# Three weight pairs computed as plain products at the start, stores on another queue, and first loads of each stage issued earlier

## The chip, the cores and the metric

The kernel runs on one core of a Trainium2 chip. The metric is the device time of one execution in microseconds (us); the median of the runs is what is compared. Before the change it is 1601.59 us, the median of three runs (1600.45 to 1611.41).

## The reference, cut to what matters

One layer of a block over 2048 tokens of width 1024, all in float32:

```
h    = rmsnorm(x) * g                                   # per token
proj = h @ w_in                                         # 1024 -> 6144 columns
q, k, v, z_att, B, C, u, z_conv, g_att, g_conv = split(proj)
att  = chunked attention: 64-token chunks, each sees itself and 8 before it, 8 heads, relative bias
ya   = (att * silu(z_att)) @ w_att_out                  # 512 -> 1024
yc   = (B * conv3_causal(C * u) * silu(z_conv)) @ w_conv_out
m    = sigmoid(g_att) * ya + sigmoid(g_conv) * yc
out  = rmsnorm(x + m @ w_out) * final_g
```

## The kernel before, in words

Every float32 matmul is done as three matmuls of rounded parts: weights and tokens are each split into a high part (a cast, on ACT) and a low part (the difference, on DVE), and high x high, high x low and low x high are summed in one PSUM bank (`passes`, L130 to L135). A *product* below is 4 contraction tiles x 3 such matmuls of 128x512, so 12 matmuls.

**The first projection.** The 6144 columns are 48 tiles of 128, taken two at a time: 24 *pairs*. The tokens are worked in two halves of 1024, each two chunks of 512. A pair in a half is a 2x2x2 block product (two column tiles, two chunks, two halves of the contraction), done by a Strassen-Winograd scheme with seven products instead of eight. `operand(p, i)` (L374) makes the weight operand i of pair p: raw weights come in two loads of 512 KB (`load_raw`), sums and differences are formed on DVE (L389 to L395), the result is split (`split_into`, L118) into one of four tiles of the pool `wr`. In the first half each operand is also stored to DRAM (L397, 512 KB, queued on SP two products later) and in the second half it is read back from there (L380). `operand_steps` (L346) makes the seven token operands of a half, in seven steps of four splits. `seq` (L536 to L543) is the list of all products by pair and i; the loop from L594 goes through it. Operands are asked for two products ahead in the first half, three in the second.

The first four pairs ("early") start before the norm is known. Products 1 and 2, which take chunk 0 alone, are computed for all four pairs from tokens that are multiplied by g only (`raw_split`, L338); their result is multiplied by the inverse norm later (`scale_early`, L588). The other five products of these pairs take normalized tokens: the sums of squares on ACT (L291), the inverse square root on DVE (`newton`, 13 small instructions), its spread over PE (L90), the multiplication in place (`normalize`, L302), the differences (`third`, L333), then the steps.

An evicted product goes to the output's handler: the gate pairs to a tanh on ACT and a store from ACT's own queue, the others to stores on SP, queued one product later by `defer` and `tick` (L108, L111). The v pairs (`ev_v`) are first transposed by PE (L431) and then split on ACT (L435) and DVE (L436) at the same point.

**Attention** (`attention`, L138) is a generator of 130 stages; its loads and stores are on GpSimd's (POOL's) queue. It starts when the first half's pairs are done (`first.close()`, L691): 64 stages are interleaved with the second half's products from the third pair on, the rest with what follows (`pump`).

**The rest**, for each half of the tokens: `half_c` takes 16 items (8 of the convolution, 8 of attention), each with a weight tile (`raw_w`, L711), two gate tiles (`gate`, L722, from the pool `gp` with three buffers) and two products over the stored inputs `mid` (`load_mid`, L717; 16 loads of 256 KB for each group of 8 items). `half_d` is the output projection of 8 token blocks, each followed by the residual, the sum of squares on ACT (L817), `newton` on DVE and the final scaling (L821) and store. The loads for each `half_c` are asked for after what stands before it in the program.

The engines' orders come from a scheduler, by priority, from the order of the program; each engine and each DMA queue then runs its list strictly in order. An instruction that waits holds everything behind it on its engine.

Of the kernel before, what the change touches and what calls it, by code (L numbers as in the profile page):

```python
# [17 lines left out]
P = 128  # L18
# [15 lines left out]
EARLY = 4  # L34

ORDER = (1, 2, 6, 5, 7, 4, 3)
REST = ORDER[2:]
# [4 lines left out]
def block_kernel(ctx, tc, xb, xt, wp_in, wy, wo, bias, ng, fg, cw, cb, out):  # L42
# [63 lines left out]
    later = []  # L106

# [230 lines left out]
    def raw_split(i, j, t):  # L338

        g = ng_sb[:, 4 * (i - 1) + j:4 * (i - 1) + j + 1]  # L340
        hi, lo = slot("rawh"), slot("rawl")
        nc.scalar.activation(hi, t, AF.Identity, scale=g)
        nc.vector.scalar_tensor_tensor(lo, t, g, hi.bitcast(F32), op0=ALU.mult, op1=ALU.subtract)
        raw_ops[i, j] = (hi, lo)

    def operand_steps(half):  # L346

        b11, b12, b21, b22 = (blocks[half, c, k] for k in range(2) for c in range(2))
        order = (1, 2, 6, 5, 7, 4, 3) if half else (1, 6, 5, 7, 2, 4, 3)
        for i in order:  # L350
# [18 lines left out]
    def load_raw(p, n):  # L369
        r = ww.tile([P, 2, 4, P], F32, tag="w", name="wraw")  # L370
        raws[p, n] = r
        nc.sync.dma_start(r, wp_in[p, n])

    def operand(p, i):  # L374
# [4 lines left out]
        if p >= NPAIR:  # L379
            nc.sync.dma_start(w.bitcast(F32), wc_d[q][i])  # L380
            return
# [15 lines left out]
        defer(2, lambda: nc.sync.dma_start(wc_d[q][i], w.bitcast(F32)))  # L397
# [14 lines left out]
    def ev_q(pr):  # L412
        def ev(g, c, t):
            for s, x in enumerate(parts(t)):
                defer(1, lambda s=s, x=x: nc.sync.dma_start(q_d[pr][s][g], x))
        return ev

    def ev_k(pr):
        def ev(g, c, t):
            for s, x in enumerate(parts(t)):  # L420
                for o in range(2):
                    r = (1 - s) * DH
                    defer(1, lambda x=x, o=o, r=r: nc.sync.dma_start(k_d[2 * pr + o][g // 2][r:r + DH, g % 2 * CH:(g % 2 + 1) * CH], x[o * DH:(o + 1) * DH]))
        return ev

    def ev_v(pr):
        def ev(g, c, t):
            def turn():
                ps = dbank("vt")
                for b in range(4):  # L430
                    nc.tensor.transpose(out=ps[:, b * P:(b + 1) * P], in_=t[:, b * P:(b + 1) * P], identity=ident)  # L431
                for b in range(2):
# [5 lines left out]
                    for h in range(2):  # L438
                        n = g % 2 * 4 + 2 * b
                        defer(1, lambda h=h, v4=v4, n=n: nc.sync.dma_start(v_d[2 * pr + h][g // 2][:, n:n + 2, :], v4[:, :, h, :]))  # L440
# [11 lines left out]
    def ev_z(pr):  # L452
        def ev(g, c, z):
            t = silu2(z)
            defer(1, lambda: nc.sync.dma_start(z_d[pr][g], t))
        return ev

    def conv_pair(b):
# [27 lines left out]
        def gated(g, c, t):  # L486
# [3 lines left out]
            if seen[g] == 2:  # L490
                for s, x in enumerate(parts(cv.pop(c))):
                    defer(1, lambda s=s, x=x: nc.sync.dma_start(mid_d[1][b][s][g], x))
# [10 lines left out]
    mixed = [C, C + 1, G + 4, C + 2, C + 3, G + 5, C + 4, C + 5, G + 6, C + 6, C + 7, G + 7]  # L503
# [3 lines left out]
    early = names[:EARLY]  # L507
    assert early == list(range(EARLY))

    def reduce_bias(h, n):  # L510
# [5 lines left out]
        def go():  # L516
# [5 lines left out]
            defer(1, lambda: nc.sync.dma_start(bias_d[h][:, n * m:(n + 1) * m], t))  # L522

        defer(3, go)

# [7 lines left out]
    main = {p: 1 for p in names}  # L533


    seq = [(p, i) for p in (2, 3, 0, 1) for i in (1, 2)]  # L536
    for p in (0, 2):
        seq += together(early[p], early[p + 1], both)
    mid0, mid1 = names[EARLY:NPAIR - 2], names[NPAIR + 2:]
    seq += [(p, i) for p in mid0 for i in ORDER]  # L540
# [3 lines left out]

    fslot = lambda name: slot(name, F32)
    nc.sync.dma_start(ng_sb, ng)
    load_x(0, 0, 0, (0, 1))
    load_raw(2, 0)
    load_x(0, 0, 0, (1, 2, 4))
    load_x(0, 0, 1)  # L550
    load_raw(3, 0)
    tok = [load_tokens(0, 0, b, fslot) for b in range(4)]
    load_x(0, 1, 0)
    load_x(0, 1, 1)
    load_raw(0, 0)
    load_raw(1, 0)
# [5 lines left out]
    t0, t1 = tiles_of(0, 0), tiles_of(0, 1)  # L562
    operand(2, 1)
    for j in range(4):
        raw_split(1, j, t0[j])
    operand(2, 2)
    for j in range(4):
        raw_split(2, j, t0[4 + j])
    acc = acc_tile()
    for b in range(4):  # L570
        sums(acc, b, tok[b])
    y0 = rsqrt_mean(acc, 4)
    tok = [load_tokens(0, 1, b, fslot) for b in range(4)]
    acc = acc_tile()
    steps = operand_steps(0)
    built = []
    pending = []
    nw = 2
    rb = {}
    x1 = None  # L580
# [7 lines left out]
    def scale_early():  # L588
        p, t, u = pending.pop(0)
        nc.vector.tensor_mul(t, t, rb[0])  # L590
        nc.vector.tensor_mul(u, u, rb[0])
        evs[p][0](0, 0, t)

    for s, (p, i) in enumerate(seq):  # L594
        half = p // NPAIR
        n = names.index(p)
        if s in (2, 3):
            load_raw(s - 2, 1)
        elif s in (15, 16):
            for k in range(2):  # L600
                load_raw(s - 13, k)
        elif s == 25 or s > 25 and half == 0 and i == 1 and n + 1 < NPAIR:
            for k in range(2):
                load_raw(names[EARLY] if s == 25 else names[n + 1], k)
        ahead = 3 if half else 2
# [3 lines left out]
        if s == 2:  # L609
            for b in range(4):  # L610
                sums(acc, b, tok[b])
            y1 = rsqrt_mean(acc, 4)
        elif s == 4:
            rb[0] = inverse(y0, fslot)
            for k in range(4):
                normalize(t0[k], k, rb[0])
        elif s == 5:
            rb[1] = inverse(y1, fslot)
            for k in range(8):
                normalize(t1[k], k, rb[1])  # L620
        elif s == 6:
            for j in range(4):
                third(0, j)
            for k in range(2):
                built.append(next(steps))
        elif s == 7:
            for k in range(4, 8):
                normalize(t0[k], k, rb[0])
        if s >= 6 and pending:
            scale_early()  # L630
        if s >= 8 and half == 0 and len(built) < 7:
# [285 lines left out]
```

## Time and profile before

| | |
|---|---|
| median of three runs | 1601.59 us (1600.45 to 1611.41) |
| the profiled execution's own time | 1607.36 us |
| its span, first to last instruction | 1605.6 us |
| PE busy | 1531.8 us, 95% of the span |
| DVE busy | 1033.1 us, 64% |
| ACT busy | 676.9 us, 42% |
| POOL busy | 155.1 us, 10% |
| mean granted TensorE clock | 0.978 |
| DMA | 417.24 MB, 260 GB/s over the span |

The profiled execution lies 5.8 us above the median; what lies around its span is 1.8 us. PE's busy time holds matmuls at half clock too, so a stretch in which PE is busy and the clock is below 1.00 has lost time as well.

### The profile page before, as it was taken

To read this page: it belongs to the slowest core of one execution; us is meant where nothing else is said; L and a number is where in the kernel's file an instruction comes from. 1 tells how busy PE (TensorE), PEld (TensorE's weight loads), DVE (VectorE), ACT (ScalarE), POOL (GpSimd) and SP (SyncE) were. 2 spreads that over 40 slices of the span, in tenths; PEclk is the share of its full clock that TensorE was granted. 3 is DMA by queue.
4 is the path that set the end of the run, shared out by engine and by line. 5 is a ranking of instruction groups with operands and counts; after the bars stand their busy time and mean duration, and the time that the engine had idled before them with its cause. 6 is when DMAs were issued, how large, how long until landed. Compare 5 with 4: busy or idle time off the path is not lost.

```text
span 1605.6 us, 21714 instructions
## 1 busy us (share of the span) xinstructions
PE 1531.8 (95%) x7344; PEld 1264.1 (79%) x7344; DVE 1033.1 (64%) x2078; ACT 676.9 (42%) x1261; POOL 155.1 (10%) x294
## 2 busy tenths in 40 slices
PE   5789999999899999999999999999999999989997
PEld 3568888888777788888888888887788877878886
DVE  4987789797668645546565555535578776665544
ACT  5443353443235323334344444425567766532211
POOL 0000000000000101111111111101233222000000
PEclk7899999999999999999999999999999999999999
DMA  9398889988887978787888898898866658277231
GB/s 350 147 349 339 323 326 340 358 329 283 315 287 249 310 250 268 232 301 248 275 293 296 281 318 264 279 310 278 294 187 205 216 181 286 86 242 262 66 105 66
DMA packets 169054, 417.24 MB, mean 260 GB/s; under 512 B 20976, under 2 KB 41456, under 8 KB 168944
## 3 DMA queue, kind: packets, MB, share of 16 engines
q1 hardware_dynamic: 138736, 329.85, 59.3%
q0 software_dynamic: 20992, 69.22, 13.5%
q10 hardware_dynamic: 9216, 16.78, 2.7%
q8 instruction: 59, 0.97, 0.2%
q14 instruction: 51, 0.42, 0.1%
HBM read 253.77 MB, written 162.00 MB: 259 GB/s over the span
## 4 chain that ended last, share of the span: by engine, by line
PE 82%; DVE 9%; DMA 5%; ACT 2%; issue 2%; SPq 0%; DVEq 0%; POOL 0%; ACTq 0%
PE ps_d L135 21%; PE ps_d L133 21%; PE ps_d L134 21%; PE po L226 4%; PE ps_t L208 3%; PE ps_s L188 3%; PE ps_d L808 3%; PE ps_d L806 3%; PE ps_d L807 3%; DMA mid<-mid 2%; DVE ps_s L194 1%; DVE wc L121 1%; DVE ptl L214 1%; DMA gl<-gate 1%; DMA wc<-wc 1%
## 5 line engine op out<-in xcount | busy, mean ns | idle before, releaser
L156 POOL DMA_DIRECT2D q<-q x128 | 66.6, 528 | 828.9 <-DMA z<-sz 541.9
L213 ACT CAST pth<-ps_t 128x640 fp32r<-128x640 f32 (+4 forms) x128 | 80.1, 626 | 124.6 <-PE ps_t L208 123.7
L198 ACT ACTIVATE pr<-ps_s,nmax 128x640 f32<-128x640 f32 (+4 forms) x128 | 93.4, 729 | 85.9 <-DVE nmax L194 81.5
L194 DVE CUSTOM_DVE_ANT_0 ps_s<-ps_s,bs 128x640 f32<-128x640 f32 (+4 forms) x128 | 95.3, 744 | 46.7 <-PE ps_s L188 46.2
L120 ACT CAST wc<-wraw 128x512 fp32r<-128x512 f32 x120 | 73.4, 621 | 120.6 <-PE ps_d L135 84.0
L200 ACT ACTIVATE pr<-pr,rs 128x640 f32<-128x640 f32 (+4 forms) x128 | 97.9, 765 | 28.1 <-DVE rs L199 27.9
L133 PE MATMUL ps_d<-mid,wy 128*128 128x512 f32 x256 | 103.3, 404 | 5.2 <-ACT wy L120 5.2
L135 PE MATMUL ps_d<-mid,wy 128*128 128x512 f32 x256 | 102.8, 402 | 2.5 <-DVE wy L121 2.5
L188 PE MATMUL ps_s<-kk,q 128*128 128x320 f32 (+1 forms) x448 | 100.0, 333 | 3.6 <-ACT pr L198 3.4
L134 PE MATMUL ps_d<-mid,wy 128*128 128x512 f32 x256 | 102.9, 402 | 0.0
L214 DVE TENSOR_TENSOR ptl<-ps_t,pth 128x640 fp32r<-128x640 f32 (+4 forms) x128 | 94.2, 736 | 9.2 <-ACT pth L213 8.7
L121 DVE TENSOR_TENSOR wc<-wraw,wc 128x512 fp32r<-128x512 f32 x120 | 81.9, 687 | 19.1 <-ACT wc L120 18.9
L208 PE MATMUL ps_t<-ident,pr 128*128 128x128 f32 x560 | 85.2, 278 | 3.4 <-DVE ptl L214 2.4
L226 PE MATMUL po<-pth,vv 128*128 128x256 f32 x336 | 81.2, 274 | 1.9 <-ACT pr L200 1.1
L226 PE MATMUL po<-ptl,vv 128*128 128x256 f32 x336 | 78.4, 281 | 1.1 <-DVE ptl L214 1.1
L188 PEld LDWEIGHTS ps_s<-kk,q 128*128 128x128 f32 x448 | 69.0, 191 | 11.8 <-ACT pr L198 9.5
L208 PEld LDWEIGHTS ps_t<-ident,pr 128*128 128x128 f32 x560 | 63.1, 141 | 15.4 <-ACT pr L200 5.4
L656 DVE TENSOR_TENSOR c<-u,ps_d 128x512 f32<-128x512 f32 x48 | 32.9, 685 | 58.8 <-PE ps_d L135 49.0
L226 PEld LDWEIGHTS po<-pth,vv 128*128 128x128 f32 x336 | 63.7, 190 | 8.9 <-ACT pth L213 4.0
L670 DVE TENSOR_TENSOR c<-v,ps_d 128x512 f32<-128x512 f32 x48 | 32.9, 686 | 56.4 <-PE ps_d L135 56.3
L666 DVE TENSOR_TENSOR v<-u,ps_d 128x512 f32<-128x512 f32 x48 | 32.9, 686 | 54.5 <-PE ps_d L135 54.4
L226 PEld LDWEIGHTS po<-ptl,vv 128*128 128x128 f32 x336 | 63.8, 190 | 5.0 <-DVE ptl L214 2.0
(360 smaller groups left out, 4213.7 us busy)
## 6 DMA issues: line engine op xcount, KB each, us to landing
wc<-wc SPq DMA_DIRECT2D x336, 512.0 KB, 4.9
wraw<-wp_in SPq DMA_DIRECT2D x50, 512.0 KB, 6.0
q<-q POOLq DMA_DIRECT2D x128, 128.0 KB, 3.6
gl<-gate SPq DMA_DIRECT2D x64, 256.0 KB, 3.5
mid<-mid SPq DMA_DIRECT2D x64, 256.0 KB, 6.2
bs<-bias POOLq DMA_DIRECT2D x32, 320.0 KB, 7.2
xt<-xt SPq DMA_DIRECT2D x32, 256.0 KB, 5.6
gate<-c ACTq DMA_DIRECT2D x32, 256.0 KB, 4.8
```

The lines of the kernel that those rows point to most:

```text
L121: nc.vector.tensor_sub(w[:, 1], src, w[:, 0].bitcast(F32))
L133: nc.tensor.matmul(ps, lhsT=w[:, 0, k, :], rhs=rh[:, cs], start=(first and k == 0), stop=False)
L134: nc.tensor.matmul(ps, lhsT=w[:, 0, k, :], rhs=rl[:, cs], start=False, stop=False)
L135: nc.tensor.matmul(ps, lhsT=w[:, 1, k, :], rhs=rh[:, cs], start=False, stop=(last and k == len(rhs) - 1))
L188: nc.tensor.matmul(ps[:, i, :m], lhsT=q[s][:, g * P:(g + 1) * P], rhs=kk[:, k1 - n + i * m:k1 - n + (i + 1) * m], start=(s == 0), stop=(s ...
L194: nc.vector.tensor_tensor_reduce(out=view, in0=view, in1=bv, scale=-0.125, scalar=3.0e38, op0=ALU.add, op1=ALU.min, accum_out=nmax)
L198: nc.scalar.activation(out, view, AF.Exp, bias=nmax, scale=-1.0, accum_out=rs)
L200: nc.scalar.activation(pr[:, :n], pr[:, :n], AF.Identity, scale=rs)
L208: nc.tensor.transpose(out=ps[:, j * P:(j + 1) * P], in_=pr[:, j * P:(j + 1) * P], identity=ident)
L213: nc.scalar.copy(hi[:, js, qs], src)
L214: nc.vector.tensor_sub(lo[:, js, qs], src, hi[:, js, qs].bitcast(F32))
L226: nc.tensor.matmul(ps[:, (g0 + a) * P:(g0 + b) * P], lhsT=vv[:, g0 + j, :], rhs=s[:, j, a * P:b * P], start=(i == 0 and s is pt[0]), stop= ...
```

## The change

Five edits.

1. *Plain pairs.* The early pairs go away. The first three pairs of the first half (`PLAIN = 3`) are computed without the Strassen scheme: for each pair, column tile n and chunk c one product of 8 contraction tiles (24 matmuls), from tokens multiplied by g only, for both chunks. The results are multiplied by the inverse norm afterwards (`scaled`). This part's order on PE, DVE and ACT is that of the program text (`manual_schedule`), and the norm, `third` and the first four steps are interleaved in it by `bulk`. Since these pairs leave no stored operands, the second half makes the operands of the three pairs anew from raw weights.
2. *Operands three ahead* in both halves, stored one product after they are asked for.
3. *Stores from POOL's queue* (`store`), until attention starts; then from SP's as before. Attention starts three pairs later in the second half, and its 64 stages are spread over what is left (133 products instead of 140).
4. *v pairs.* The split follows the transposes one product later.
5. *First loads sooner.* The `mid` inputs and the first item's weights and gates of each `half_c` are asked for in the work before it; `gp` has five buffers and is there before the first projection ends; the final stores of `half_d` are queued one step later. The second half of the tokens starts with the pairs G+3 and G+4, then the three plain ones; the gate pairs G+5 to G+7 come last.

The core of the diff:

```diff
+PLAIN = 3
+    queue = [nc.gpsimd]
+    def store(dst, src):
+        queue[0].dma_start(dst, src)
     def operand(p, i):
-        if p >= NPAIR:
+        if p >= NPAIR and q >= PLAIN:
             nc.sync.dma_start(w.bitcast(F32), wc_d[q][i])
             return
...
-        defer(2, lambda: nc.sync.dma_start(wc_d[q][i], w.bitcast(F32)))
+        if p < NPAIR:
+            defer(1, lambda: store(wc_d[q][i], w.bitcast(F32)))
     def ev_v(pr):
...
+                defer(0, lambda: split(ps))
+            def split(ps):
-    order = [[G, G + 1, G + 2, G + 3, *mixed, *range(Q, Q + 8)]]
-    order.append([G, G + 1, *mixed, *range(Q, Q + 8), G + 2, G + 3])
+    order = [[*range(G, G + 4), *conv_gate(G + 4, G + 5, G + 6, G + 7), *range(Q, Q + 8)]]
+    order.append([G + 3, G + 4, *range(G, G + PLAIN), *conv_gate(), *range(Q, Q + 8), G + 5, G + 6, G + 7])
+    def weights0(p, n, k):
+        w = wtile("w0")
+        wops0[p, n, k] = w
+        split_into(w, raws[p, n][:, k])
+    def scaled(p, n, c, src):
+        t = src if src.space != PSUM else e("c")
+        nc.vector.tensor_mul(t, src, rb[c])
+        evs[p][n](c, c, t)
+    with tc.manual_schedule(engines={mybir.EngineType.PE, mybir.EngineType.DVE, mybir.EngineType.Activation}):
...
+        for q, (p, n, c) in enumerate(plain):
+            if q in (5, 7):
+                rb[(q - 5) // 2] = inverse(ry[(q - 5) // 2], fslot)
+            ps = dbank("ps_p")
+            for k in range(2):
+                passes(ps, wops0[p, n, k], [raw_ops[c, 4 * k + j] for j in range(4)], slice(0, CH), k == 0, k == 1)
...
-        ahead = 3 if half else 2
+        ahead = 3
-        elif n > NPAIR + 1:
-            want = (s - (NPAIR + 2) * 7) * 64 / (20 * 7)
+        elif n == NPAIR + 1 + PLAIN and i == 3:
+            first.close()
...
+            queue[0] = nc.sync
+        elif ab:
+            want = (s - s0) * 64 / (len(seq) - s0)
+        if n == NPAIR + 2 + PLAIN + 8 and i == 1:
+            conv_stack.close()
+            gp = pool("gp", 5)
+        if n == 2 * NPAIR - 1 and i == 5:
+            mids = {c: [load_mid(1, b, c) for b in range(4)] for c in (0, 1)}
+            made = make_c(0, ITEMS_C[0])
-    gp = pool("gp", 3)
...
+    def next_half(n):
+        if n == 9:
+            nxt["mids"] = {c: [load_mid(1, b, c) for b in range(4)] for c in (2, 3)}
+        elif n == 13:
+            nxt["made"] = make_c(1, ITEMS_C[0])
```

Three places in the engines' orders. First ACT at the very start; `xt` are the tokens whose squares are summed, `rawh` the high parts of the tokens times g that PE takes first, `wc` and `w` weight operands. Before:

```order
L120 ACT_TABLE_LOAD
L120 CAST wc<-wraw 128x512 x4
L291 ACTIVATE xt,acc<-xt 128x512 x4
L342 ACTIVATE rawh<-xs,ng_sb 128x512
L291 ACTIVATE xt,acc<-xt 128x512
```

and now:

```order
L123 ACT_TABLE_LOAD
L123 CAST w_601<-wraw 128x512
L345 ACTIVATE rawh<-xs,ng_sb 128x512 x4
L123 CAST w_620<-wraw 128x512
L345 ACTIVATE rawh<-xs,ng_sb 128x512 x4
L123 CAST w_639<-wraw 128x512
L123 CAST w_642<-wraw 128x512
```

Four weight casts from two loads and four sums of squares stood ahead of the first token operand; now one cast does.

Second DVE at the passage from the first `half_d` to the second `half_c`; `wy` is the low part of that stage's first weights, the small instructions on `ry`, `ra` and `rv` are the inverse square root of an output block, and L821 (now L860) is its final scaling. Before, the end of the last block's chain:

```order
L75 TENSOR_TENSOR ra<-ry,rv 128x1
L76 SCALAR_TENSOR_TENSOR ra<-ra,ry 128x1
L77 SCALAR_TENSOR_TENSOR ry<-ra,ry 128x1
L821 SCALAR_TENSOR_TENSOR y<-y,ry,fg_sb 128x512 x2
L121 TENSOR_TENSOR wy<-wraw,wy 128x512
L773 TENSOR_TENSOR wo<-wraw,wo 128x512
```

and now, where the last block's chain begins:

```order
L76 SCALAR_TENSOR_TENSOR ry<-ra,ry 128x1
L860 SCALAR_TENSOR_TENSOR y<-y,ry,fg_sb 128x512 x2
L124 TENSOR_TENSOR wy<-wraw,wy 128x512
L851 SCALAR_TENSOR_TENSOR y<-ps_d,y 128x512 x2
L82 TENSOR_TENSOR rv<-ssq 128x1
L83 TENSOR_SCALAR rv<-rv 128x1
```

The first `wy` stood behind the last block's chain and now stands ahead of it.

Third SP's queue in the middle of the first `half_c`, where the 16 `mid` loads of the attention items are queued; `gate_5_1` is the gate tile of item 5, second chunk (the last number of a name is a buffer's). Before, the end of the `mid` loads:

```order
L717 DMA mid<-mid_2_1_1_238 128x512
L717 DMA mid<-mid_3_0_1_242 128x512
L717 DMA mid<-mid_3_1_1_246 128x512
L711 DMA wraw<-wy 128x512
L722 DMA gl<-gate_5_1_206 128x512
L722 DMA gl<-gate_6_0_209 128x512
```

and now, their beginning:

```order
L545 DMA gl<-gate_4_1_202 128x512
L545 DMA gl<-gate_5_0_205 128x512
L813 DMA wraw<-wo 128x512
L545 DMA gl<-gate_5_1_206 128x512
L540 DMA mid<-mid_0_0_0_217 128x512
L540 DMA mid<-mid_0_1_0_221 128x512
```

The gate of item 5 stood behind all 16 `mid` loads and now stands ahead of them.

More of the change, by code (lines that the diff above doesn't have):

```diff
@@ L561, in block_kernel @@
         nc.tensor.matmul(idle, lhsT=warm[:, :P], rhs=warm, start=True, stop=True)
[L562 to L574, printed above, removed]
+    tt_ = [tiles_of(0, c) for c in range(2)]
@@ L608, in block_kernel @@
             nw += 1
[L609 to L631, printed above, removed]
-            if s % 2 == 0 or i not in built:
-                built.append(next(steps))
+        if half == 0 and len(built) < 7 and s:
+            built.append(next(steps))
         if n == 5 and i == 1:
@@ L644, in block_kernel @@
         ps = dbank("ps_d")
[L645 to L646 removed]
+        passes(ps, wops.pop((p, i)), [ops[half, i, j] for j in range(4)])
         tick()
@@ L738, in half_c @@
         att_mids = {}
[L740 to L744 removed]
+        for n_, (i, d) in enumerate(ITEMS_C):
+            raw, gl = made
+            if n_ + 1 < len(ITEMS_C):
+                made = make_c(hf, ITEMS_C[n_ + 1])
             w = wtile("wy")
```

222 lines of the change are left out of this document (131 added, 91 removed).

## The prediction, made before the changed kernel ran

> **What bounds the kernel now.** I read the page's head first, then the busy times by stage, then what PE waits for in the stages where it is not busy.
>
> ```profile
> PE 1531.8 (95%) x7344; PEld 1264.1 (79%) x7344; DVE 1033.1 (64%) x2078; ACT 676.9 (42%) x1261; POOL 155.1 (10%) x294
> ...
> core 0: us, PE busy (x) PEld busy (x) DVE busy (x) ACT busy (x) POOL busy (x), PEclk, DMA share, GB/s
> 17.00:130.00 113.00, 90.96 (x345) 69.93 (x346) 97.13 (x177) 56.00 (x108) 0.00 (x0) 0.87 0.76 285
> 130.00:415.00 285.00, 285.00 (x1262) 235.97 (x1262) 231.64 (x423) 114.87 (x204) 0.00 (x0) 1.00 0.90 328
> 415.00:560.00 145.00, 132.40 (x564) 103.89 (x563) 97.84 (x164) 52.85 (x101) 7.62 (x14) 0.98 0.82 283
> 560.00:1075.00 515.00, 514.70 (x2598) 436.12 (x2597) 269.85 (x547) 203.72 (x390) 71.69 (x134) 1.00 0.84 277
> 1075.00:1100.00 25.00, 21.36 (x95) 17.50 (x94) 9.65 (x16) 7.44 (x13) 0.94 (x2) 0.86 0.87 317
> ...
> 1145.00:1170.00 25.00, 21.72 (x113) 18.58 (x113) 11.26 (x22) 11.11 (x18) 5.49 (x11) 0.86 0.73 242
> 1170.00:1400.00 230.00, 223.58 (x1281) 186.91 (x1280) 173.59 (x398) 153.12 (x279) 55.60 (x104) 1.00 0.62 199
> 1400.00:1425.00 25.00, 20.41 (x80) 15.92 (x79) 13.92 (x41) 6.62 (x15) 0.55 (x1) 0.86 0.53 170
> ```
>
> PE sets the time: from 130 to 415 us and from 560 to 1075 us it is busy throughout at full clock, so only what adds or removes matmuls counts there. Elsewhere it stands idle: 22.0 us of 17 to 130 us, 12.6 us of 415 to 560 us, and 3.6, 3.3 and 4.6 us in three stretches of 25 us whose clock is also down to 0.86. These stretches are what can be won.
>
> At the start PE waits for its operands, and DVE makes them:
>
> ```profile
> PE ps_d L133 <- ACT rawh L342: 10.1, 1, 10.1
> PE ps_d L133 <- ACT t60h L126: 6.4, 1, 6.4
> PE ps_d L133 <- ACT t40h L126: 6.2, 1, 6.2
> PE ps_d L133 <- ACT wc L120: 5.7, 1, 5.7
> ...
> 45.00:80.00 35.00, 26.66 (x101) 19.86 (x100) 34.77 (x58) 16.97 (x31) 0.00 (x0) 0.85 0.32 124
> ```
>
> From 45 to 80 us DVE is full (34.77 of 35 us), while PE has done the eight raw products and waits for step operands.
>
> **The change, part by part. The start.** Durations and landmarks:
>
> ```profile
> 6.73 1.14 ACT L120 CAST wc<-wraw 128x512 fp32r<-128x512 f32 x2 [4.71 <-DMA wraw<-wp_in]
> 12.90 1.14 ACT L120 CAST wc<-wraw 128x512 fp32r<-128x512 f32 x2 [5.03 <-DMA wraw<-wp_in]
> 13.94 0.62 ACT L291 ACTIVATE xt<-xt 128x512 f32<-128x512 f32 x1
> 16.40 0.70 ACT L342 ACTIVATE rawh<-xs,ng_sb 128x512 fp32r<-128x512 f32 x1
> ...
> 46.92 5.38 DVE L302 SCALAR_TENSOR_TENSOR xs<-xs,ng_sb,rb 128x512 f32<-128x512 f32 x8
> 53.43 2.49 DVE L333 TENSOR_TENSOR xs<-xs 128x512 f32<-128x512 f32 x4
> ...
> 129.61 0.39 PE L135 MATMUL ps_d<-t33h,wc 128*128 128x512 f32 x1
> 129.84 0.39 PE L133 MATMUL ps_d<-t10h,wc 128*128 128x512 f32 x1
> ```
>
> The first weights are there at 6.73 us, but ACT takes the second weights (12.90) and four sums ahead of the first token operand (16.40). Back to back, a DVE instruction takes 0.66 us with two operations ((5.38 - 0.74)/7, by the duration of one) and 0.60 us with one ((2.49 - 0.68)/3); a matmul follows the last after 0.227 us (129.84 - 129.61, rounded). The fifth pair's first matmul (t10) is at 129.84 us: the first four pairs take until then.
>
> In the changed order the first loads are the same. ACT casts the first weights at 6.73 and makes the first token operand by 7.9; PE starts at about 8. DVE makes two low weights and eight low operands (2 x 0.60 + 8 x 0.66 = 6.5 us from 7.3, so 13.8), and PE ends the first 24 matmuls at about 15. From there I follow each engine. PE: six more products, 6 x 24 x 0.227 = 32.7, and one spread of the norm, 0.6: 48.3 us, if it is fed; the eight operands of chunk 1 end at 20.4 on DVE and are first wanted at 20.5. DVE: it cannot begin the norm's backlog before ACT has squared the second chunk's tokens. ACT turns to these eight after the first norm's spread, at 37.6, and takes 8 x 0.61: 42.5; `newton` follows with 13 small instructions at about 0.16: 44.6. From there to the last token operand (t33l) stand 16 instructions of two operations and 76 of one: 16 x 0.66 + 76 x 0.60 = 56.2, so 100.8 us. PE in that time does five plain products and a whole Strassen pair, (120 + 84) x 0.227 = 46.3, held back by PSUM banks and operands that wait for DVE; its last product follows the last operands, 2.7 us after a predecessor that ends at about 102: 105 us. That is again four pairs, 129.8 - 105 = 25 us sooner, with the 36 extra matmuls (8.2 us) in it: PE works during DVE's backlog. Bounds: fed perfectly after 15 us, 348 matmuls end at 94 with the two spreads 95, a gain of 35; if every DVE instruction costs its full duration (0.74 and 0.68) the backlog takes 63.5, and if the first 24 matmuls run at half clock (0.43, below) 5 us more: 116, a gain of 14. I take 25.
>
> *The second half's share of it.* The operands of three pairs are made again: 11 instructions a pair on DVE (four sums, seven low parts), 6.6 us in a pair's 84 x 0.227 = 19.1 us. From 560 to 1075 us DVE is busy 269.85 of 515 us, so PE's own work hides it; were DVE full there, 20 us would show. Attention three pairs later meets PE at 514.70 of 515 us either way. Both: nothing.
>
> **v pairs, and three ahead.**
>
> ```profile
> ACT vst L435 <- PE vt L431: 32.5, 8, 7.5
> ...
> PE ps_d L135 <- DVE wc L121: 7.8, 9, 2.1
> ...
> 500.00:545.00 45.00, 40.69 (x163) 30.76 (x163) 42.63 (x71) 25.94 (x47) 1.80 (x4) 0.96 0.67 242
> ```
>
> Between 400 and 600 us ACT stands 32.5 us before v splits while PE has not transposed yet; behind it in ACT's order stand weight casts, behind these DVE's low parts, and PE waits 7.8 us for those. The later split and the third operand in hand end that. Of the 12.6 us, 4.3 lie in 500 to 545 us where DVE is full (42.63 of 45) with the second half's steps, which nothing changes; 8.3 are left, some more with the clock. I take 6, bounds 0 and 9.
>
> **First loads.**
>
> ```profile
> 1076.19 5.40 DMA mid<-mid
> 1081.61 6.90 DMA mid<-mid
> ...
> 1091.61 0.62 ACT wy L120
> ...
> 1092.27 0.80 PE ps_d L133
> ...
> 1097.33 0.43 PE ps_d L134
> ...
> 1138.09 7.83 DMA mid<-mid
> ...
> 1145.99 10.17 DMA gl<-gate
> ...
> 1412.69 0.69 DVE L812 SCALAR_TENSOR_TENSOR y<-ps_d,y 128x512 f32<-128x512 f32 x1 [4.75 <-PE ps_d L808]
> ...
> 1416.68 1.41 DVE L821 SCALAR_TENSOR_TENSOR y<-y,ry,fg_sb 128x512 f32<-128x512 f32 x2
> 1418.01 0.68 DVE L121 TENSOR_TENSOR wy<-wraw,wy 128x512 fp32r<-128x512 f32 x1
> ```
>
> Three stalls, each followed by matmuls at 0.43 instead of 0.227 us. At 1092 the first weights come behind the `mid` loads; the `mid` loads now start three products earlier, over 8 us, which covers the 3.6 us for which PE stood idle. At 1156 a gate comes 10.17 us late behind the next `mid` loads; it now stands ahead of them. At 1418 `wy` comes behind the last block's chain; it now stands ahead, where DVE sits idle (4.75 us). Each costs its idle time (3.6, 3.3, 4.6) and the half clock: 1092.27 to 1097.8 is some 13 matmuls, 13 x 0.20 = 2.6; I take 2.5 for each. All three: 19.0. The Trainium skill's page "TensorE: Matmul & The Clock Gate" (Part 1, the HAM clock gate) has the clock fall after an idle window of about 3.4 us; by that the stall of 3.3 us would cost itself alone and the sum be 16.5. The trace has 0.86 around that stall as around the others, so the rows decide. For the late first weights and gates I leave 2 us: 17, bounds 6 and 19.
>
> **Stores on POOL's queue.**
>
> ```profile
> wc<-wc SPq DMA_DIRECT2D x100, 512.0 KB, 4.8
> ...
> L160 POOL DMA_DIRECT2D kk<-k x16: 572/575/582, 545.4 to 1205.3; - x16
> ...
> DMA to landing us min/median/max: 3.1/5.8/11.0
> ```
>
> From 120 to 400 us a 512 KB transfer of an operand from SP lands in 4.8 us (median). The nearest row for POOL is `kk`, a load of 512 KB with an issue of 0.575 us: median landing 5.8, longest 11.0 over all `kk`. A `wr` tile must be back after four products, 4 x 12 x 0.227 = 10.9 us, less 1.3 for the split and 0.6 for the issue: 9.0. The median is well inside: nothing lost; nothing gained either, since PE is full from 130 to 415 us. With fewer stores SP's loads are not held behind stores, which is in the terms above. The final stores that are queued a step later change nothing behind the last matmul.
>
> **Sum.** 25 + 6 + 17 = 48; I take 3 off for waits that appear in their place, as each queue has a next-latest instruction: 45. Against the profiled execution's own 1607.4 that is 1562; it lies 5.8 above the median, so 1601.6 - 45 = 1557 us. With all low bounds (14 + 0 + 6 - 3 = 17) it is 1585, with all high (35 + 9 + 19) 1539; mostly between 1543 and 1574.
>
> **Rivals.**
> *The start stays bound by DVE.* The work on DVE is hardly less; if banks and order make PE wait for it as before, four pairs end at 120 and the start gives 10: 33 - 3 = 30, 1572 us. For it: DVE is full from 45 to 80 us now, and in my count from 45 to 100. Against: PE has 288 matmuls that need no step.
> *The stalls of the passages come back elsewhere.* Gates and `mid` loads still share one queue; if the three stalls give 0 and the rest holds, 31 - 3 = 28: 1574 us. Against: the order shows each late instruction ahead of what held it.
> *Both* (10 + 6 - 3 = 13): 1589 us, so no change by my bound, which is 1% (16 us, about what a measurement of this kernel can tell from none).
> *Slower: POOL's stores land late.* Each us of landing over 9.0 costs every stored product of the first half a quarter of it: 147 x 0.25 = 37 us. At `kk`'s longest landing, 11.0, that is 73: 1557 + 73 = 1630 us. It eats the gain from 10.2 us on, and is slower by 1% from 10.7. For it: 147 stores of 512 KB run while the DMA engines are 0.90 busy. Against: the median 5.8. The Trainium skill's page "SBUF — State Buffer" (section "SBUF: two separate sides") gives a mechanism that would do this, GpSimd unable to write descriptors while DVE holds the shared port. The row of `kk` issues (572 to 582 ns, up to 1205 us) shows no such delay, with DVE busy 173.59 of the 230 us from 1170 us on.
>
> **Numbers.** Forecast 0.58, start bound by DVE 0.14, passages 0.12, both 0.09, POOL late 0.07. Faster by over 1% (below 1586): 0.58 + 0.13 + 0.11 + 0.02 = 0.84, the last three being those cases' shares below it; slower by over 1%: 0.06 of the POOL case; within: the rest, 0.10. The range 1543 to 1586 holds nearly all of the forecast and most of the two partial cases, and leaves out about 0.2.
>
> **What would show it.** Right: in the changed profile PE's first matmul after the warm-up comes near 8 us and the first matmul of the second Strassen pair near 105 us; the stages after it are full until 430 us; the idle around the passages is gone and the clock there is 1.00; store landings on POOL's queue stay under 9 us. Wrong: PE idle between 50 and 100 us of more than 15 us; PE waiting for weight casts that wait for `wr` tiles from 130 to 415 us; or idle time on PE in the second half's first five pairs, where DVE makes operands again.

## The result, and the profile after

The changed kernel takes 1617.93 us (median of 7 runs, 1609.78 to 1621.42) against 1604.74 us for the kernel before (7 runs, 1600.45 to 1611.41). The ratio is 1.0077, with a 95% interval of 1.005 to 1.0105: slower by 0.8%, less than the 1% the prediction counted as no change, but more than its own uncertainty. Forecast were 1557 us and a range up to 1586.

To see where the time went, I take the same piece of work in both traces and ask when it begins. The first matmul of a weight pair multiplies `t10h`; these rows of the timeline of TensorE (start, duration, engine, line, operation, out<-in) are those of the fifth, the twentieth and the twenty-seventh pair of the changed kernel, and after them those of the twentieth and twenty-seventh of the kernel before (its fifth, at 129.84, stands in the prediction):

```profile
117.66 0.39 PE L136 MATMUL ps_d<-t10h,wc 128*128 128x512 f32 x1
444.31 0.39 PE L136 MATMUL ps_d<-t10h,wc 128*128 128x512 f32 x1
593.33 0.39 PE L136 MATMUL ps_d<-t10h,wc 128*128 128x512 f32 x1
```

```profile
416.39 0.39 PE L133 MATMUL ps_d<-t10h,wc 128*128 128x512 f32 x1
574.86 0.39 PE L133 MATMUL ps_d<-t10h,wc 128*128 128x512 f32 x1
```

With the first `wy` product of each half (1092.27 and 1414.69 before, 1106.31 and 1425.43 after) and the last matmul (1596.67 and 1607.93), that makes six stretches, in us of the two profiled executions (spans 1605.6 and 1617.2):

| stretch | before | after | difference |
|---|---|---|---|
| start to fifth pair | 129.84 | 117.66 | -12.2 |
| fifth to twentieth pair | 286.55 | 326.65 | +40.1 |
| twentieth to twenty-seventh pair | 158.47 | 149.02 | -9.5 |
| twenty-seventh pair to first `wy` product | 517.41 | 512.98 | -4.4 |
| to the second half's first `wy` product | 322.42 | 319.12 | -3.3 |
| to the last matmul | 181.98 | 182.50 | +0.5 |

Five of the six got shorter or hardly moved, though the start won only half of what was forecast. The second, 40 us lost where the kernel before was full, decides the sign. The windows of the changed kernel over stretches that the prediction showed for the kernel before (columns: busy time and count of PE, PEld, DVE, ACT, POOL, then granted clock, DMA share, GB/s):

```profile
17.00:130.00 113.00, 98.14 (x405) 79.48 (x404) 81.28 (x149) 55.58 (x111) 7.60 (x14) 0.91 0.60 218
130.00:415.00 285.00, 261.42 (x1105) 210.80 (x1104) 205.91 (x386) 99.73 (x183) 73.75 (x138) 0.97 0.79 286
415.00:560.00 145.00, 135.60 (x587) 109.38 (x586) 107.66 (x180) 58.58 (x109) 67.05 (x115) 0.96 0.86 303
...
1400.00:1425.00 25.00, 24.26 (x118) 20.10 (x117) 13.62 (x41) 7.10 (x14) 1.09 (x2) 1.00 0.32 108
```

From 130 to 415 us PE was busy 285.00 of 285; now 261.42, at 0.97 of its clock. It does 1105 matmuls there in place of 1262. What it waits for, and what VectorE waits for, in that window:

```profile
PE ps_d L136 <- ACT sz L454: 8.8, 4, 3.4
PE ps_d L136 <- ACT c L405: 7.3, 4, 2.8
PE ps_d L136 <- ACT hi L411: 3.8, 2, 3.4
PE ps_d L136 <- DVE u L731: 3.6, 4, 1.8
```

```profile
DVE s L391 <- DMA wraw<-wp_in: 61.3, 13, 7.2
```

In the kernel before the same instruction, one line in 130 to 415 us, waited next to nothing:

```profile
DVE s L389 <- DMA wraw<-wp_in: 3.2, 5, 0.9
```

PE's rows name ScalarE and VectorE, but these are the last links only. Line 391 is the sum `s1 = a21 + a22`, from which operand 6 of a pair is made. One instance, from the timelines of SyncE's queue, VectorE, ScalarE and PE of the changed kernel:

```profile
233.51 3.81 SPq L374 DMA_DIRECT2D wraw<-wp_in  x2
```

```profile
237.38 0.69 DVE L726 TENSOR_TENSOR v<-u,ps_d 128x512 f32<-128x512 f32 x1
237.98 0.69 DVE L124 TENSOR_TENSOR wc<-wraw,wc 128x512 fp32r<-128x512 f32 x1
244.18 0.69 DVE L391 TENSOR_TENSOR s<-wraw 128x512 f32<-128x512 f32 x1 [5.52 <-DMA wraw<-wp_in]
244.79 0.68 DVE L730 TENSOR_TENSOR c<-v,ps_d 128x512 f32<-128x512 f32 x1
```

```profile
245.57 0.63 ACT L405 ACTIVATE c<-c 128x512 f32<-128x512 f32 x1 [4.30 <-DVE c L730]
```

```profile
246.22 0.47 PE L136 MATMUL ps_d<-t10h,wc 128*128 128x512 f32 x1 [2.40 <-ACT c L405]
246.53 0.41 PE L137 MATMUL ps_d<-t10l,wc 128*128 128x512 f32 x1
246.76 0.60 PE L138 MATMUL ps_d<-t10h,wc 128*128 128x512 f32 x1
247.16 0.63 PE L136 MATMUL ps_d<-t11h,wc 128*128 128x512 f32 x1
247.59 0.63 PE L137 MATMUL ps_d<-t11l,wc 128*128 128x512 f32 x1
```

The two loads of a later pair's raw weights are issued from 233.51 to 237.32, as soon as buffers of `ww` come free. VectorE is through with what stands ahead of the sum at 238.67, 1.4 us later, before they have landed, and stands 5.52 us. Behind it stand the evictions of products 7 (L730 and L731), 4 (L735) and 3 (L739), which hold the three banks of `ps_d`. PE does the products it still has banks for, then stands 2.40 us before the next pair's first product, and then does some matmuls 0.43 us apart in place of 0.227. Such a stop comes before nearly every pair: 15 pauses of 0.18 to 3.43 us in the stretch. Over the whole stretch from the fifth to the twentieth pair PE's busy time is 300.66 of 326.65 us:

```profile
117.66:444.31 326.65, 300.66 (x1269) 242.79 (x1268) 230.88 (x426) 113.17 (x206) 89.17 (x167) 0.97 0.81 293
```

so 26.0 us are pauses, and the other 14.1 (300.66 less the 286.55 that the same work takes undisturbed) are slow matmuls around them: some 44 of them are 0.43 us apart, which is 44 x 0.20 = 9 us, and the rest are mostly the matmuls next to the pauses. The Trainium skill's page "PSUM — Partial Sum Buffer" (section "Engine vs sequencer instructions") calls the queues of ScalarE, VectorE and GpSimd strict FIFO; the 5.52 us for which ready evictions stand behind the sum agree.

### The profile page after: what moved, and what is told of

It reads as the page before. It is cut to its first block, busy times and chain, and to the rows that moved or that the text cites. A ratio compares the mean times of both kernels' runs of the same rounds, so it can differ in the third digit from the quotient of the medians.

```text
span 1617.2 us, 21868 instructions
## 1 busy us (share of the span) xinstructions
PE 1540.8 (95%) x7380; PEld 1272.9 (79%) x7380; DVE 1035.7 (64%) x2081; ACT 687.7 (43%) x1282; POOL 303.2 (19%) x561
## 4 chain that ended last, share of the span: by engine, by line
PE 55%; DMA 10%; DVE 7%; ACT 2%; issue 2%; POOL 0%; SPq 0%; DVEq 0%; ACTq 0%; POOLq 0%
PE ps_d L136 12%; PE ps_d L138 12%; PE ps_d L137 12%; PE po L229 3%; PE ps_d L847 3%; PE ps_d L845 3%; PE ps_d L846 3%; PE ps_t L211 3%; PE ps_s L191 3%; DMA mid<-mid 3%; DMA wc<-wc 2%; DMA wraw<-wp_in 2%; DVE ptl L217 1%; DMA wraw<-wo 1%; DVE ps_s L197 1%
## 5 line engine op out<-in xcount | busy, mean ns | idle before, releaser
L109 POOL DMA_DIRECT2D wc<-wc x147 | 79.2, 539 | 358.7 <-DVE wc L124 302.2
L391 DVE TENSOR_TENSOR s<-wraw 128x512 f32<-128x512 f32 x24 | 16.6, 693 | 83.6 <-DMA wraw<-wp_in 83.6
```

## The experiments

**Theory A**: VectorE reaches the sum too soon after its load was issued, stands there, and PE's banks are not emptied. **Rival B**: the stores land late from GpSimd's queue, and with three operands ahead the four `wr` tiles do not come back. **Rival C**: two queues at work slow the DMA as such. Landmarks of all kernels are in a table at the end of this part; PE's and VectorE's waits are quoted where the verdict rests on them.

### The sum held back, stores left where they are

```diff
-    s_pool = fp("s", 2)
+    s_pool = fp("s", 1)
...
-        s1 = s_pool.tile([P, 4, P], F32, tag="s1", name="s1")
+        s1 = s_pool.tile([P, 4, P], F32, tag="s1b" if p in (names[NPAIR - 1], names[NPAIR + 1]) else "s1", name="s1")
```

> Edit: the sum a21+a22 for operand 6 has one buffer for every pair (a second one only for the two pairs whose products are interleaved), so VectorE cannot compute it until the pair before has made operand 5 from its own. Stores stay on GpSimd's queue and three operands stay ahead. Theory A (VectorE stands in order behind this sum, which waits for raw weights not yet landed; the evictions behind it hold PE): VectorE's waits for the raw weights fall from 83.6 us to under 10, the stretch from the first matmul of the fifth pair to that of the twentieth from 326.7 us to 287 to 292, and the kernel from 1617.9 to about 1580 us (1573 to 1590). Rival B (the stores land too late on GpSimd's queue, and with three operands ahead the four weight tiles do not come back in time): nothing that B rests on is touched, 1612 to 1622 us. Rival C (the DMA queues as such are slower with two queues at work): 1612 to 1622 us as well.

Measured: 1572.12 us, a ratio of 0.979 (0.9756 to 0.9825) to the kernel before. The window, and then all that is left of VectorE's waits for raw weights in the whole run:

```profile
130.00:415.00 285.00, 285.00 (x1263) 236.06 (x1262) 235.77 (x428) 116.13 (x207) 93.70 (x175) 1.00 0.91 333
```

```profile
DVE s L391 <- DMA wraw<-wp_in: 7.3, 2, 3.7
```

PE is full again at full clock, and the stretch takes 286.56 us, as before the change. Stores, queues and operands ahead are untouched, so B and C fall. The kernel came out a little below A's own range (1573 to 1590): the stretch after it got 5 us shorter as well (143.98 in place of 149.02).

### All stores on SyncE's queue

```diff
-    queue = [nc.gpsimd]
+    queue = [nc.sync]
```

> Edit: the changed kernel with all its stores back on SyncE's queue. The order then has the sum 1 to 5 rows ahead of its use in most pairs, in place of 9 to 24. Theory A: most of the 40 us come back, VectorE's waits for raw weights under 15 us, 1580 to 1590 us. Rival B: the same time, 1575 to 1590 us, but then with the sum's waits as before. If neither the queue nor the sum matters: 1612 to 1622 us.

Measured: 1578.11 us, ratio 0.9823 (0.9787 to 0.9859), a little under A's range; 286.55 us from the fifth to the twentieth pair, and 13.9 us of VectorE's waits for raw weights in the whole run. So the queue of the stores did bring the loss about, though not by their landing. From the twentieth to the twenty-seventh pair this kernel takes 153.19 us, against 149.02 with the stores on GpSimd's queue and 143.98 with the sum held back besides. There the new queue wins: 4.2 us as the kernel stands, and at most 9.2, since the second comparison changes the sum's buffer too.

### The kernel before, with nothing changed but the stores' queue

```diff
-        defer(2, lambda: nc.sync.dma_start(wc_d[q][i], w.bitcast(F32)))
+        defer(2, lambda: store(wc_d[q][i], w.bitcast(F32)))
```

(and so for the other stores of the first half and of `bias`, with `store` on GpSimd's queue until attention begins).

> Edit: the kernel before with nothing changed but the queue of the first half's stores and of the bias stores: GpSimd's in place of SyncE's. Its order has the sum 8 to 24 rows ahead of its use. Theory A: the stretch of the fifth to the twentieth pair goes from 286.6 to about 320 us, the kernel from 1604.7 to 1630 to 1645 us, with 50 us or more of VectorE waiting for raw weights. Rival B (three operands ahead with late stores): here only two are ahead, so little changes, 1603 to 1612 us. Rival C: 1620 us or more, but with waits of weight casts for stores and not of the sum for raw weights.

Measured: 1639.99 us, ratio 1.0212 (1.0173 to 1.0251), within A's numbers; the stretch takes 320.75 us against 286.55 (the start is 5.9 us longer as well). From the fifth to the twentieth pair VectorE waits

```profile
DVE s L393 <- DMA wraw<-wp_in: 60.1, 14, 6.9
```

One part of the change alone, with two operands ahead and no plain pair, brings the loss. The order of VectorE's instructions shows how. In the kernel before, the sum `s_2648` follows the evictions of products 7, 4 and 3 (L670, L671, L675, L679):

```
320 L670 TENSOR_TENSOR c_2419<-v,ps_d 128x512
321 L121 TENSOR_TENSOR wc<-wraw,wc 128x512
322 L671 TENSOR_TENSOR u<-u,ps_d 128x512
323 L675 TENSOR_TENSOR u<-u,ps_d 128x512
...
326 L679 TENSOR_TENSOR v<-v,ps_d 128x512
...
332 L389 TENSOR_TENSOR s_2648<-wraw 128x512
```

With the stores on the other queue it stands ahead of them (L674, L675, L679, L683 are the same four):

```
320 L393 TENSOR_TENSOR s_2648<-wraw 128x512
321 L674 TENSOR_TENSOR c_2419<-v,ps_d 128x512
322 L675 TENSOR_TENSOR u<-u,ps_d 128x512
323 L125 TENSOR_TENSOR wc<-wraw,wc 128x512
324 L399 TENSOR_TENSOR wraw<-wraw 128x512
325 L679 TENSOR_TENSOR u<-u,ps_d 128x512
...
330 L683 TENSOR_TENSOR v<-v,ps_d 128x512
```

No line of VectorE's program was edited. Only the queue of some stores was, and the scheduler set the sum elsewhere.

### Two operands ahead in the first half

```diff
-        ahead = 3
+        ahead = 3 if half else 2
```

> Edit: the changed kernel with two operands ahead in the first half in place of three; the sum stands as far ahead of its use as in the changed kernel (9 to 24 rows). Theory A: no gain in the stretch of the fifth to the twentieth pair, 1612 to 1622 us. Rival B: the weight tiles come back in time, the 40 us return, 1575 to 1590 us.

Measured: 1613.11 us, ratio 1.0043 (1.0024 to 1.0062); 321.07 us for the stretch, VectorE's waits for raw weights 74.6 us in the run. The third operand is not the cause, and B falls by this too.

### The sum early, with stores on SyncE's queue

```diff
+        if half == 0 and i == 4 and n + 2 < NPAIR - 2:
+            early_sum(names[n + 2])
```

(`early_sum` is the sum taken out of `operand`; the raw weights of the pair two ahead are loaded at product 7, in place of those of the next pair at product 1; the stores are on SyncE's queue).

> Edit: the changed kernel with all stores on SyncE's queue, as in the run on the queue alone, but with the sum for operand 6 written, and its raw weights' load too, most of a pair earlier: in the order the sum then stands 7 to 20 rows ahead of its use in ten of the first sixteen pairs, in place of 1 to 5 in most. Theory A (the place of the sum costs, whatever queue the stores use): VectorE's waits for raw weights 25 to 50 us in place of 13.9, the stretch from the fifth to the twentieth pair 295 to 315 us in place of 286.6, the kernel 1585 to 1610 us. Rival H (the loss needs the stores on GpSimd's queue; the early sum alone is covered): 287 to 290 us, 1575 to 1582.

Measured: 286.56 us for the stretch, 13.6 us of waits in the run, 1582.94 us in one run. Theory A missed as I had put it; the numbers are rival H's, nearly. An early sum alone costs nothing. The timelines say why. From the end of the load's issue to the moment when VectorE comes to the sum it is here some 6 us (median of the 14 pairs of the stretch), about as in the kernel before (6.5), since the load moved with the sum; in the changed kernel it is some 2 us, and with the sum held back 10 to 18. With the stores on SyncE's queue, too, the few sums that come sooner wait: one 2.4 us after its load's issue stands 1.89 us in this kernel, one 4.0 us after it stands 2.41 us in the first kernel with all its stores on that queue. So what counts is not how far the sum stands ahead of its use, but how soon it comes after its own load, and that is A as it has to be put. No run brings most sums to 2 us after their loads with the stores on SyncE's queue, so that GpSimd's queue adds nothing to the loss is argued from these rows. From issue to landing such a load takes 6.6 us in the changed kernel (median, 130 to 415 us):

```profile
wraw<-wp_in SPq DMA_DIRECT2D x26, 512.0 KB, 6.6
```

### The start: weight casts ahead of the tanh

The prediction missed the start by 13 us. VectorE's waits in the changed kernel between 45 and 118 us:

```profile
DVE w L124 <- ACT w L123: 4.4, 2, 2.6
DVE wc L124 <- ACT wc L123: 1.8, 1, 1.8
DVE c L719 <- PE ps_d L138: 1.5, 1, 1.5
```

The next two kernels, and the three after them, stand on the one with the sum held back.

```diff
             else:
+                if c and p + 1 < PLAIN:
+                    for k in range(2):
+                        cast0(p + 1, n, k)
                 for _ in range({5: 2, 6: 3, 7: 3, 8: 3, 9: 2}.get(q, int(q > 9))):
```

(`cast0` is the first half of `weights0`, the cast on ScalarE; VectorE's low part stays behind.)

> Edit, on the kernel with one buffer for the sum: in the plain products, ScalarE casts the next pair's weights (four casts, at the sixth and seventh product of the second kind) ahead of the tanh of the finished products instead of behind it. Theory D (the start falls short of the forecast because VectorE, full with its backlog, is held by weight casts that stand in ScalarE's order behind a tanh, which itself waits for VectorE): of the 6.1 us in which VectorE waits for such casts some 4 go, the fifth pair's first matmul comes at 114 to 116 us in place of 119.1, the kernel at 1567 to 1570 us in place of 1572. Rival E (VectorE simply has more to do in the backlog than counted): 118 to 120 us, 1571 to 1574.

Measured: 116.47 us in place of 119.08 for the fifth pair, 1569.54 us, ratio 0.9763 (0.9745 to 0.978). VectorE's waits for these casts between 45 and 118 us fell from 6.1 to 3.0 us. That is theory D's direction, with 2.6 us of the 3 to 5 expected; the kernel with the loads spread, whose start is not edited, has its fifth pair at 118.05, so about 1 us of the 2.6 may be no effect of the edit.

### The start: no tanh in the plain products

```diff
-        evs[p][n](c, c, t)
+        nc.sync.dma_start(gate_d[n][p][c], t)
```

> Edit, on the kernel with one buffer for the sum: the tanh of the twelve plain products is left out (so the gates of three pairs are not what the reference computes), and their stores are issued by SyncE, so that nothing on ScalarE waits there for VectorE's scaled products. Theory D: the fifth pair's first matmul at 110 to 115 us in place of 119.1, and VectorE's waits for weight casts between 45 and 115 us under 2 us in place of 6.1. Rival E: 117 to 120 us.

Measured: fifth pair at 111.45 us, 7.6 sooner, and VectorE's waits for weight casts between 45 and 118 us are down to

```profile
DVE wc L124 <- ACT wc L123: 1.2, 2, 0.7
```

Both numbers are D's: two engines, each in order, stand for each other in turn (ScalarE's tanh for VectorE's product, VectorE's low part for ScalarE's cast). The tanh is left out, so ScalarE also has 12 times 0.63 us less to do, and SyncE issues the stores; the one run does not part these.

### The second half's attention values in four steps

```diff
-            if i == 1 and d == 4:
+            if hf == 0 and i == 1 and d == 4:
                 for c in cs:
                     att_mids[c] = [load_mid(0, b, c) for b in range(4)]
+            elif hf and i == 1 and 3 <= d < 7:
+                for c in cs:
+                    att_mids.setdefault(c, []).append(load_mid(0, d - 3, c))
```

> Edit, on the kernel with one buffer for the sum: the sixteen loads of the attention values for the second half's output products are issued four at a time over four steps, not sixteen in one step. Theory F (the third passage's stall has only moved: behind these 4 MB the raw output weights land late, VectorE waits for their cast, and the eviction that frees PE's bank stands behind it): the 4.5 us wait of PE for that eviction goes, from the second half's first output-side product to the next stage 89 us in place of 93.4, 1567 to 1569 us in all. Rival G (the loads wait for free tiles whatever their order): 93 us, 1571 to 1573.

In the kernel it stands on, PE has one wait of size between the second half's first `wy` product and the next stage:

```profile
PE ps_d L136 <- DVE part L788: 4.5, 1, 4.5
```

With the loads spread it is gone, that stretch takes 87.70 us in place of 93.44, and the kernel 1569.07 us, ratio 0.9761 (0.9745 to 0.9776). Theory F holds: the third passage's stall had not gone, it had moved. It is the same mechanism once more: an eviction on VectorE stands behind an instruction that waits for a load.

### Two operands ahead, with the sum held back

The edit is that of the run with two ahead above.

> Edit, on the kernel with one buffer for the sum: two operands ahead in the first half in place of three. If the third operand in hand carries a good part of what the stretch from the twentieth to the twenty-seventh pair won (158.5 us before, 144.0 with three), that stretch gets 4 to 8 us longer and the kernel 1576 to 1580 us; if the later v split and the stores' queue carry it, 144 to 146 us and 1571 to 1574.

Measured: 147.16 us in place of 143.98, 1576.15 us, ratio 0.9797 (0.9772 to 0.9822). The third operand is worth 3.2 us, less than the 4 to 8 expected.

### Together

```diff
-        if n == 2 * NPAIR - 1 and i == 5:
-            mids = {c: [load_mid(1, b, c) for b in range(4)] for c in (0, 1)}
-            made = make_c(0, ITEMS_C[0])
+        if n == 2 * NPAIR - 1 and i == 6:
+            made = make_c(0, ITEMS_C[0])
+            mids = {c: [load_mid(1, b, c) for b in range(4)] for c in (0, 1)}
```

(besides the held sum, the earlier casts and the spread loads).

> Edit: the three that gained or may, together: one buffer for the sum, the weight casts ahead of the tanh in the plain products, the second half's attention values loaded in four steps; besides, the first weights of the output products are loaded ahead of the values beside them. If the parts add: 1572 - 2.6 - 5.7 + 0 = 1564 us (1561 to 1568), the fifth pair at 116.5 us, the second half's output products 87 to 88 us; if the stretch between the first output product and the next stage falls into its longer form (169 to 170 us in place of 164 to 166), 1568.

Measured: 1565.11 us, ratio 0.9733 (0.9719 to 0.9748) to the kernel before, so faster than both and within the 1561 to 1568 expected. That the first weights are loaded ahead of the values shows no gain: the stretch before the first `wy` product is 2 us longer (514.44 against 512.18). The head of its page:

```profile
PE 1520.6 (97%) x7380; PEld 1262.0 (81%) x7380; DVE 1039.6 (66%) x2081; ACT 690.2 (44%) x1282; POOL 303.2 (19%) x561
```

The stretches of all kernels, in us, as in the table of the result:

| kernel | start to 5th | 5th to 20th | 20th to 27th | 27th to `wy` | to second `wy` | to last matmul |
|---|---|---|---|---|---|---|
| before | 129.84 | 286.55 | 158.47 | 517.41 | 322.42 | 181.98 |
| before, stores on GpSimd's queue | 135.72 | 320.75 | 151.97 | 517.10 | 327.22 | 182.58 |
| after | 117.66 | 326.65 | 149.02 | 512.98 | 319.12 | 182.50 |
| after, two ahead | 117.45 | 321.07 | 149.51 | 512.72 | 316.10 | 180.69 |
| after, stores on SyncE's queue | 117.43 | 286.55 | 153.19 | 512.58 | 315.20 | 182.05 |
| the same, sum and load early | 117.53 | 286.56 | 153.18 | 512.64 | 320.14 | 181.99 |
| after, sum held back | 119.08 | 286.56 | 143.98 | 512.18 | 316.14 | 182.49 |
| the same, casts first | 116.47 | 287.78 | 143.98 | 511.89 | 320.30 | 182.10 |
| the same, no tanh | 111.45 | 287.74 | 144.29 | 512.49 | 321.19 | 181.72 |
| the same, loads spread | 118.05 | 288.37 | 142.92 | 512.38 | 319.68 | 176.75 |
| the same, two ahead | 117.65 | 287.30 | 147.16 | 512.40 | 315.82 | 182.76 |
| together | 115.71 | 288.38 | 144.41 | 514.44 | 317.38 | 176.51 |

## Why the prediction was wrong

**The step that failed is "Stores on POOL's queue": "nothing lost; nothing gained either, since PE is full from 130 to 415 us".** I costed the stores that were moved, and in the median they did as forecast: 147 of 512 KB land in 5.3 us. The longest took 10.8, over the 9 that I had set as the mark, and ScalarE stood 33.4 us in 16 waits for them. That is not what PE lost: with the sum held, stores land no sooner in the median (5.5 us, longest 9.3), ScalarE still waits 8.8 us in 6 of them, and PE does not stop from the fifth to the twentieth pair. So the slower rival (late stores) did not come about. Their rows, landing times and issues (ns, minimum, median, maximum):

```profile
wc<-wc POOLq DMA_DIRECT2D x147, 512.0 KB, 5.3
```

```profile
L109 POOL DMA_DIRECT2D wc<-wc x147: 532/532/679, 89.5 to 549.5; - x147
...
DMA to landing us min/median/max: 2.9/5.3/10.8
```

No issue took longer than 0.68 us beside a busy VectorE, so the port rule of the "SBUF — State Buffer" page of the Trainium skill (section "SBUF: two separate sides"), weighed in the prediction, does not show here.

What I did not cost is what taking them off SyncE's queue does to the instructions that I took to be unmoved. The sum's place on VectorE changed, and it cost 40.1 us where I had put 0: shown by taking that one thing away (the sum held back: 286.56), and by making that one change to the kernel before (320.75). A full PE says that nothing can be won there; I read it as if nothing could be lost. The prediction's own list of what would show it wrong held "PE waiting for weight casts that wait for `wr` tiles" for this window. The stops that came were for banks.

**The same term was wrong on the other side.** From the twentieth to the twenty-seventh pair the stores' queue wins 4.2 us in the changed kernel (153.19 to 149.02) and 6.5 in the kernel before (158.47 to 151.97), which I had also put at nothing. With the stores on SyncE's queue PE waits there 5.9 us for weights (4.0 for casts, 1.9 for low parts); with them on GpSimd's and the sum held, 0.3.

**The start: mechanism right, size off.** PE started at 8.45 us against a forecast of 8, at full clock. The gain was 12.2 us, not 25, and under the lower bound of 14. The mis-sized term is DVE's backlog, taken as 56.2 us back to back. It took 68.3, and the last token operand ended at 114.0, not 100.8; of these 13 us VectorE stood about 10 (4.4 and 1.8 of them for weight casts behind a tanh). The rival "the start stays bound by DVE" had 10 and was nearer. Without the tanh the gain is 18.4. From 50 to 100 us PE stood idle 14.0 us; the prediction's mark of 15 for a wrong step was set too wide to catch it.

**v pairs and three ahead: right in sign, low.** 6 forecast, 9.5 measured, 14.5 with the sum held. Of these 14.5 us the third operand is worth 3.2, and the queue and the held sum together 9.2 (153.19 to 143.98). If these add, some 2 us are left for the later v split, which was not tried by itself.

**First loads: about half.** 17 forecast; the last three stretches gave 4.4 + 3.3 - 0.5 = 7.2, with the sum held 11.0. The stall of the third passage moved to the middle of the next stage, as the rival "the stalls of the passages come back elsewhere" had it, and spreading the loads took back 5.7. In the first passage PE comes to the first `wy` product without a pause, but then stands 1.9 and 1.7 us for attention's probabilities. ScalarE and VectorE have just stood 4.95 and 3.54 us for `wy` loads there; that the one comes of the other was only argued.

**The sum.** With its 40.1 us replaced by nothing the profiled execution would have taken 1617.2 - 40.1 = 1577 us, so 29 less than before where I had 45: inside the range of 1543 to 1586, as the kernel with the sum held back is (1572.12). Part of that is luck, since the start and the first loads together fell 23 us short, while the stretch from the twentieth to the twenty-seventh pair won more than forecast. One thing stays open: I do not know why the scheduler sets the sum earlier when stores leave SyncE's queue. That it does is plain from the order; its reason was not tried.

## What to carry to other kernels

Moving transfers to another queue, with a scheduler that orders every engine, is an edit of every engine's order: compare the order of the engine that empties PSUM, also where PE is full and nothing seems to change. For each instruction on it that waits for a load, ask how long after the load's issue it comes, and what stands behind it. One buffer less can be the cheapest way to hold such an instruction back.

## What the runs showed of the hardware

**Short pauses halve PE's clock, though not always.** After the pause of 2.40 us (above, 246 us) PE ran some 3 us at half clock. From the fifth to the twentieth pair of the changed kernel the six pauses of 2.40 to 3.43 us are each followed by six to eight matmuls 0.43 us apart, and the nine of 0.18 to 1.99 us by none; that makes about a quarter of the 40 us. The length of the pause alone does not decide it: in the kernel before with its stores moved, a pause of 1.84 us is followed by eight such matmuls and one of 2.50 us by none. Two kernels of the last part have the same short stop for `vv` in the second passage, with 1.8 and 1.9 us idle in ten:

```profile
1131.80:1141.80 10.00, 8.17 (x49) 6.73 (x48) 4.57 (x10) 4.12 (x7) 3.71 (x7) 1.00 0.59 187
```

```profile
1130.12:1140.12 10.00, 8.11 (x40) 6.93 (x39) 3.98 (x9) 3.61 (x6) 0.88 (x2) 0.84 0.57 202
```

The first (sum held) keeps its clock, the second (casts first) drops to 0.84. The Trainium skill's page "TensorE: Matmul & The Clock Gate" (Part 1, the HAM clock gate) has the clock fall after an idle window of about 3.4 us, which is free-running. A window that does not begin with the pause would fit different outcomes for like pauses, which no run here shows to be the reason; but pauses of 1.84 and 2.40 us, shorter than 3.4, were enough here, and the measurement decides. The stretch between the two halves' first `wy` products takes 315 to 317 us in some kernels and 319 to 321 in others with no edit in it. Between the two kernels shown it differs by 4.2 us, of which 2.6 are PE's busy time (306.62 and 309.24 us for the same work) and 1.5 its pauses; what makes a kernel fall on one side was not tried.

**A separate queue for stores is neither good nor bad by itself.** The Trainium skill's page "Perfetto Trace Analysis" (section "DMA Optimizations") says that it may make sense to give loads one engine's queue and stores another's. Here that was worth 6.5 us in one stretch and cost 34.2 in another of one and the same kernel (the kernel before with its stores moved). With the sum held back it cost nothing in that other stretch (286.56 us).
